# A hybrid decoder layer on one core: the list scheduler's machine model is exchanged

## The chip, the core and the metric

The kernel runs on one core of a Trainium2 chip. The metric is the device time of one execution, in microseconds (us). Of the kernel before there are three runs, with a median of 2636.88 us (2635.72 to 2638.27), and one profiled execution. A core has TensorE (PE, matrix products), VectorE (DVE), ScalarE (ACT) and GpSimd (POOL); SyncE (SP) issues all DMAs of this kernel. Each engine works through its own list of instructions in order; what one engine needs of another it waits for on semaphores.

## The reference

One layer of a decoder, in fp32, for 2048 prompt tokens and 8 x 8 sample tokens that share all weights (model width 1024). Cut to what matters:

```python
q, k, v, u = split(rmsnorm(x, g_mix) @ w_in)        # 1024 -> 1280
attn_o = window_attention(q, k, v, sinks)            # 8 heads x 64, 2 kv heads, window 128, ALiBi
pool_o = pool_mix(u, w_pool) * pool_scale            # causal means over 2, 4, 8, 16 tokens
x = x + concat(attn_o, pool_o) @ w_out
h = rmsnorm(x, g_cross)
p = softmax((h @ w_cq) @ mem_k.T / 16)               # 4 heads x 256, 256 memory tokens
x = x + (p @ mem_v) @ w_co
h = rmsnorm(x, g_ffn)
x = x + square(relu(h @ w_up)) @ w_down              # hidden width 4096
y = rmsnorm(x, g_final)
```

The sample tokens have their own window cache, pooling state and memory cache. For the prompt, mem_k and mem_v are computed from mem_prompt. Keys, values and pooling states are returned too.

## The kernel before

**Precision.** Each fp32 operand of a large product is split into a rounded part "hi" and a remainder "lo", and the product is three passes: hi x hi, hi x lo, lo x hi (L111 to L113 in `mm3`, L280 to L282 in `dense`). The split of a weight tile is made on the core: a DMA brings 512 KB into a staging tile (L131), ScalarE rounds it (L132), VectorE subtracts (L133). That is done 330 times.

**Weights.** The class `Stream` holds a list of all weight tiles in the order of use. `pump` emits the loads and splits ahead of their use, up to five tiles, as far as staging tiles (six) and weight tiles (twelve) are free.

**Activations** lie transposed: features in the partitions, tokens in the columns. The tokens are worked through in three superblocks of two blocks each, of 384 columns (320 or 256 in the last). All tiles are allocated once and handed out by small free lists while the program is traced, so who reuses which buffer after whom is fixed by the traced program.

**Stages.** The prologue warms TensorE up (14 small matmuls of an identity with a tile of ones, L367), splits the memory tokens, computes mem_k and mem_v, and folds w_cq into mem_k and w_co into mem_v, writing the folded matrices to DRAM. Then for each superblock: the input projection interleaved with the window attention, w_out, cross attention with the folded matrices, the MLP in eight groups of 512 hidden channels. In the last superblock the sample tokens have an attention (`attn_sample`) and a cross attention (`sample_cross`) of their own, which reads the sample caches by 512 KB transfers.

**The dense loop.** `dense` goes over output chunks of 128 channels and the two blocks. A chunk for one block is 24 passes into one of four PSUM banks (`MM`). `order` says which chunk of which block comes when: the first `head` chunks run for block 0 and then for block 1, likewise the last `tail`.

**Norms.** For each finished chunk of a residual, VectorE adds (L892, L1093 or L1164), ScalarE squares (L205) and GpSimd adds the square to an accumulator (L206). `Norm.fin` then sums the accumulator over the partitions with a matmul of ones (L214), takes Ln and Exp (L217, L218), three operations on VectorE (L219 to L221), and `Norm.apply` makes the normalised hi and lo parts in eight pieces (L232, L233, L235; the last on VectorE and GpSimd by turns). `fin` is put in a list `later` and traced one chunk after the block's last chunk. Its matmul is the only instruction of the kernel with `keep_in_program_order`, which puts it behind the TensorE instruction that was traced just before it; what is traced after it may still be put ahead of it.

**Attention.** For each tile of 128 queries and each kv head: scores (L676), mask and maximum (L677), Exp, division, transposes by TensorE (L707), probabilities times values (L724, L725). These steps are written as stages with lags, and the generators `attn` and `ug` (the input projection) are traced in turns by `mix`.

**What sets the order.** The traced program is a first order. When the `TileContext` closes, the framework's scheduler makes each engine's list: it is a list scheduler that plays the program on a model of the machine, and takes, for an engine that is free, the earliest traced instruction whose inputs and buffers are ready in that model. So an instruction that waits in the model is passed by others that are traced behind it. How far the lists differ from the traced order depends on what the model takes for the length of each instruction and transfer. The context is opened in `kernel` at L1317.

## Time and profile before

| | |
|---|---|
| median of three runs | 2636.88 us |
| profiled execution, span from first to last instruction | 2632.9 us |
| busy: TensorE, VectorE, ScalarE, GpSimd | 2565.7, 1304.3, 982.1, 665.8 us |
| mean granted TensorE clock | 0.992 of full speed |
| moved by DMA | 244.76 MB, 93 GB/s over the span |

The profile gives no time of its own for the profiled execution outside its span; the span is 4.0 us under the median of the runs. In a row of the timeline stand the start, the length, the engine, the line of the kernel, the operation, the tile it writes and the tiles it reads, how many instructions are merged in the row, and in brackets the idle time before it with what ended it. Matmuls overlap, so a matmul's length in a row is not the distance to the next one; that distance is read from the starts. A row of stretches gives each engine's busy time between two points of the span. "Granted clock" is the share of TensorE's full clock in a stretch.

### The profile page before, as it was taken

To read this page: it belongs to the slowest core of one execution; us is meant where nothing else is said; L and a number is where in the kernel's file an instruction comes from. 1 tells how busy PE (TensorE), PEld (TensorE's weight loads), DVE (VectorE), ACT (ScalarE), POOL (GpSimd) and SP (SyncE) were. 2 spreads that over 40 slices of the span, in tenths; PEclk is the share of its full clock that TensorE was granted. 3 is DMA by queue.
4 is the path that set the end of the run, shared out by engine and by line. 5 is a ranking of instruction groups with operands and counts; after the bars stand their busy time and mean duration, and the time that the engine had idled before them with its cause. 6 is when DMAs were issued, how large, how long until landed. Compare 5 with 4: busy or idle time off the path is not lost. (4 is left out here: it accounts for less than half of the span.)

```text
span 2632.9 us, 39258 instructions
## 1 busy us (share of the span) xinstructions
PE 2565.7 (97%) x15753; PEld 2461.6 (93%) x15753; DVE 1304.3 (50%) x2283; ACT 982.1 (37%) x1923; POOL 665.8 (25%) x723
## 2 busy tenths in 40 slices
PE   8899999999999999999999999999999999999998
PEld 8799989999999999997999999999999669999998
DVE  7567453533333367936363333334766646344334
ACT  6666342422222244824342222223354434322231
POOL 2215322311111153433241111113324214111111
PEclk9999999999999999999999999999999999999999
DMA  7843211211111123131111111112414473222210
GB/s 276 257 130 104 71 47 64 73 65 64 65 65 64 56 70 108 55 123 57 65 63 60 63 64 64 65 57 70 141 60 146 178 269 117 81 81 83 87 57 37
DMA packets 92539, 244.76 MB, mean 93 GB/s; under 512 B 16772, under 2 KB 31556, under 8 KB 91204
## 3 DMA queue, kind: packets, MB, share of 16 engines
q1 hardware_dynamic: 92356, 242.25, 27.0%
q8 instruction: 123, 2.02, 0.3%
q14 instruction: 60, 0.49, 0.1%
HBM read 219.53 MB, written 22.69 MB: 92 GB/s over the span
## 5 line engine op out<-in xcount | busy, mean ns | idle before, releaser
L280 PE MATMUL mm<-act,w 128*128 128x384 f32 (+2 forms) x2784 | 903.0, 324 | 2.6 <-ACT act L631 1.6
L281 PE MATMUL mm<-act,w 128*128 128x384 f32 (+2 forms) x2784 | 897.7, 322 | 0.7 <-DVE act L632 0.5
L282 PE MATMUL mm<-act,w 128*128 128x384 f32 (+2 forms) x2784 | 897.1, 322 | 1.2 <-DVE w L133 1.2
L132 ACT CAST w<-f 128x1024 fp32r<-128x1024 f32 x330 | 346.0, 1050 | 734.7 <-PE mm L112 459.7
L133 DVE TENSOR_TENSOR w<-f,w 128x1024 fp32r<-128x1024 f32 x330 | 425.3, 1294 | 304.7 <-ACT w L132 304.5
L111 PE MATMUL mm<-act,w 128*128 128x384 f32 (+2 forms) x1728 | 552.4, 320 | 9.3 <-ACT w L132 7.6
L113 PE MATMUL mm<-act,w 128*128 128x384 f32 (+2 forms) x1728 | 549.2, 318 | 0.5 <-DVE w L133 0.5
L112 PE MATMUL mm<-act,w 128*128 128x384 f32 (+2 forms) x1728 | 548.9, 318 | 0.0
L280 PEld LDWEIGHTS mm<-act,w 128*128 128x128 f32 x2784 | 527.6, 189 | 7.4 <-issue 2.6
L281 PEld LDWEIGHTS mm<-act,w 128*128 128x128 f32 x2784 | 527.3, 189 | 7.3 <-issue 2.6
L282 PEld LDWEIGHTS mm<-act,w 128*128 128x128 f32 x2784 | 527.2, 189 | 2.0 <-DVE w L133 1.7
L1131 POOL TENSOR_TENSOR t<-t 128x384 f32<-128x384 f32 (+2 forms) x192 | 216.2, 1126 | 1039.5 <-ACT t L1130 1039.5
L1164 DVE TENSOR_TENSOR x<-mm,x 128x384 f32<-128x384 f32 (+2 forms) x384 | 199.8, 523 | 327.9 <-PE mm L113 327.9
L111 PEld LDWEIGHTS mm<-act,w 128*128 128x128 f32 x1728 | 327.2, 189 | 11.3 <-ACT w L132 7.6
L112 PEld LDWEIGHTS mm<-act,w 128*128 128x128 f32 x1728 | 327.1, 189 | 1.0
L113 PEld LDWEIGHTS mm<-act,w 128*128 128x128 f32 x1728 | 327.0, 189 | 0.8 <-DVE w L133 0.8
L206 POOL TENSOR_TENSOR t<-t,t 128x384 f32<-128x384 f32 (+2 forms) x161 | 191.4, 1190 | 344.7 <-ACT t L205 311.7
L1134 DVE TENSOR_TENSOR act<-t,act 128x384 fp32r<-128x384 f32 (+2 forms) x192 | 102.9, 536 | 305.4 <-ACT act L1133 305.4
L1133 ACT CAST act<-t 128x384 fp32r<-128x384 f32 (+2 forms) x192 | 93.4, 487 | 235.3 <-POOL t L1131 235.3
L205 ACT ACTIVATE t<-x 128x384 f32<-128x384 f32 (+2 forms) x140 | 68.3, 498 | 153.1 <-DVE x L1093 75.6
L1130 ACT ACTIVATE t<-mm 128x384 f32<-128x384 f32 (+2 forms) x192 | 88.3, 460 | 93.2 <-PE mm L282 91.9
L111 PE MATMUL mm<-w,act 128*128 128x512 f32 x288 | 117.1, 409 | 3.0 <-ACT w L132 2.7
(187 smaller groups left out, 2211.8 us busy)
## 6 DMA issues: line engine op xcount, KB each, us to landing
f<-in_wup SPq DMA_DIRECT2D x96, 512.0 KB, 3.5
f<-in_wdn SPq DMA_DIRECT2D x96, 512.0 KB, 3.5
f<-in_win SPq DMA_DIRECT2D x30, 512.0 KB, 3.7
f<-a_s SPq DMA_DIRECT2D x24, 512.0 KB, 3.3
f<-b_s SPq DMA_DIRECT2D x24, 512.0 KB, 4.2
x<-in_x SPq DMA_DIRECT2D x6, 1536.0 KB, 7.0
f<-in_wco SPq DMA_DIRECT2D x16, 512.0 KB, 5.5
f<-in_cmk SPq DMA_DIRECT2D x16, 512.0 KB, 4.5
```

The costliest lines, as they stand in the source:

```text
L111: nc.tensor.matmul(ps, Wh(k), Hh(k), start=first and i == 0, stop=False)
L112: nc.tensor.matmul(ps, Wh(k), Hl(k), start=False, stop=False)
L113: nc.tensor.matmul(ps, Wl(k), Hh(k), start=False, stop=final and i == last)
L132: nc.scalar.copy(th[:], r[:, 0:1024])
L133: eng.tensor_tensor(tl[:], r[:, 0:1024], f32(th[:]), ALU.subtract)
L206: self.add.tensor_tensor(self.acc[:, 0:n], self.acc[:, 0:n], t[:, 0:n], ALU.add)
L280: nc.tensor.matmul(ps[:, 0:n], w8(th)[:, k, :], hi(b, k), start=k == 0, stop=False)
L281: nc.tensor.matmul(ps[:, 0:n], w8(th)[:, k, :], lo(b, k), start=False, stop=False)
L282: nc.tensor.matmul(ps[:, 0:n], w8(tl)[:, k, :], hi(b, k), start=False, stop=k == 7)
L1131: nc.gpsimd.tensor_tensor(q[:, 0:n], r[:, 0:n], r[:, 0:n], ALU.mult)
L1134: nc.vector.tensor_tensor(lo, q[:, 0:n], f32(hi), ALU.subtract)
L1164: nc.vector.tensor_tensor(bl.x(m), ps[:, 0:n], bl.x(m), ALU.add)
```

## The change

The `TileContext` is opened with `schedule_with_timeline_sim=True`. The list scheduler then plays the traced program on the framework's timeline model of the machine instead of its default model. Instructions, tiles, buffers, engines and the dependences between instructions stay as they are. The lists of all five engines, the order in which SP issues its DMAs, and the places of the waits can differ.

```diff
-    with tile.TileContext(nc) as tc:
+    with tile.TileContext(nc, schedule_with_timeline_sim=True) as tc:
         tile_hybrid_step_kernel(tc, io)
```

## The prediction

> **What bounds the kernel now.** I read the page first (who is busy), then the busy time by stage (where TensorE is not), then the list of TensorE's waits (what holds it up), then the timeline at the longest wait and at the start.
>
> ```profile
> span 2632.9 us, 39258 instructions
> PE 2565.7 (97%) x15753; PEld 2461.6 (93%) x15753; DVE 1304.3 (50%) x2283; ACT 982.1 (37%) x1923; POOL 665.8 (25%) x723
> 0.00:230.00 230.00, 211.53 (x1341) 196.90 (x1342) 167.10 (x354) 154.99 (x331) 58.39 (x82) 0.99 0.58 193
> 470.00:930.00 460.00, 459.64 (x2650) 459.38 (x2651) 165.51 (x228) 122.99 (x193) 79.47 (x70) 1.00 0.19 64
> 1350.00:1830.00 480.00, 480.00 (x2771) 479.95 (x2770) 178.74 (x254) 131.70 (x212) 86.79 (x78) 1.00 0.19 63
> 1920.00:2010.00 90.00, 84.01 (x579) 78.36 (x579) 67.04 (x193) 58.17 (x165) 37.67 (x64) 0.94 0.29 100
> 2010.00:2210.00 200.00, 189.41 (x1301) 151.69 (x1300) 106.06 (x183) 81.59 (x152) 56.11 (x61) 0.99 0.53 188
> 2210.00:2600.00 390.00, 389.96 (x2907) 389.69 (x2906) 159.60 (x253) 113.45 (x197) 71.06 (x70) 1.00 0.21 73
> 2600.00:2633.00 33.00, 22.43 (x152) 20.46 (x151) 14.79 (x34) 6.92 (x16) 4.16 (x5) 0.89 0.19 73
> ```
>
> After the bounds and the length of a stretch stand the busy times of PE, PEld, DVE, ACT and POOL, then granted clock, DMA share, GB/s. TensorE is idle for 2632.9 - 2565.7 = 67.2 us in all. The three long dense stretches, 460 + 480 + 390 = 1330 us, hold 0.4 us of it: half of the kernel has nothing that an order can fill. At the end, 10.6 us of 33 are the drain behind the last matmuls. What an order can touch is in the other stages: prologue, attention, the stage boundaries, the sample group's cross attention. There TensorE waits for this:
>
> ```profile
> PE aux L214 <- POOL t L206: 20.7, 9, 3.7
> PE mm L111 <- ACT w L132: 10.3, 3, 7.6
> PE aux L676 <- DVE st L677: 2.8, 6, 0.9
> ```
>
> The three numbers are the total in us, the times, and the longest. Of the second row 7.6 us are the wait for the first data. The first row is the largest: the matmul that sums a norm's squares over the partitions, held up nine times, by up to 3.7 us, by GpSimd's last addition.
>
> **The part that decides: order.** The diff changes no instruction, only the model of the machine on which the scheduler finds out what is ready when. So I look for places where the present order shows that its model was wrong about this chip. A list scheduler that knew of a wait would have put ready work into it. At the longest wait it did not:
>
> ```profile
> 466.16 0.33 PE L281 MATMUL mm<-act,w 128*128 128x384 f32 x1
> 466.34 0.34 PE L282 MATMUL mm<-act,w 128*128 128x384 f32 x1
> 470.36 0.91 PE L214 MATMUL aux<-t,ones 128*128 128x384 f32 x2 [3.69 <-POOL t L206]
> 470.82 0.63 PE L280 MATMUL mm<-act,w 128*128 128x384 f32 x1
> 463.86 4.00 DVE L133 TENSOR_TENSOR w<-f,w 128x1024 fp32r<-128x1024 f32 x2
> 467.78 0.55 DVE L1093 TENSOR_TENSOR x<-mm,x 128x384 f32<-128x384 f32 x1
> 468.25 1.21 DVE L133 TENSOR_TENSOR w<-f,w 128x1024 fp32r<-128x1024 f32 x1
> 468.42 0.52 ACT L205 ACTIVATE t<-x 128x384 f32<-128x384 f32 x1 [3.39 <-DVE x L1093]
> 464.78 2.00 POOL L206 TENSOR_TENSOR t<-t,t 128x384 f32<-128x384 f32 x1
> 469.09 1.22 POOL L206 TENSOR_TENSOR t<-t,t 128x384 f32<-128x384 f32 x1 [2.31 <-ACT t L205]
> ```
>
> The 24 passes of the first w_up chunk end at 466.34, L214 follows in its traced place at 470.36, and the next chunk starts right behind it: block 0's activations had been in use for 24 passes, so it was ready. The chain that L214 waits for is DVE's residual add (467.78, itself behind two weight subtractions), ACT's square, POOL's addition. The model of before must have had that chain done earlier, or TensorE later. The start shows the same from the other side:
>
> ```profile
> 1.01 0.29 POOL masks.py:199 TENSOR_SCALAR_AFFINE_SELECT ident<-ident 128x128 f32<-128x128 f32 x1
> 7.57 0.58 PE L111 MATMUL mm<-act,w 128*128 128x256 f32 x1 [7.57 <-ACT w L132]
> ...
> 9.43 0.41 PE L112 MATMUL mm<-act,w 128*128 128x256 f32 x1
> 9.64 5.62 PE L367 MATMUL aux<-ident,ones 128*128 128x128 f32 x28
> 15.02 0.36 PE L113 MATMUL mm<-act,w 128*128 128x256 f32 x1
> 15.22 0.28 PE L111 MATMUL mm<-act,w 128*128 128x256 f32 x1
> 15.34 0.29 PE L112 MATMUL mm<-act,w 128*128 128x256 f32 x1
> 8.69 2.46 DVE L380 SCALAR_TENSOR_TENSOR act<-x,vec,act 128x256 fp32r<-128x256 f32 x6
> 11.93 1.22 DVE L133 TENSOR_TENSOR w<-f,w 128x1024 fp32r<-128x1024 f32 x1
> ```
>
> The warm-up passes (L367) are traced ahead of every weight matmul and need only the identity, which is complete at 1.01 + 0.29 = 1.30 us. Five L111/L112/L113 matmuls (first and last shown) were put ahead of them, so they run from 9.64 to 15.0, in front of real work, where from 1.3 to 7.57 they would be free.
>
> **Term 1, warm-up.** If it goes first, L113 need not wait till 15.02. It is then paced by DVE: the last input piece is there at 8.69 + 2.46 = 11.15 and the second chunk's subtraction ends at 11.93 + 1.22 = 13.15. The first chunk's 19 remaining passes (0.12 us each, 15.22 to 15.34) would be over by about 11.5, the second is bound by 13.15; now the first ends at 15.02 + 19 x 0.12 = 17.3. Gain 17.3 - 13.15 = 4.2 us; the bounds are 0 (the model again takes the identity for late) and the whole 5.4 us from 9.64 to 15.02.
>
> **Term 2, the norm sums.** Upper bound 20.7 us. Lower bound 0.4 us per wait, by what is late next: a gap filled at L214 brings TensorE sooner to the block whose norm was being summed. After 470.82 come three chunks of block 0, 72 passes x 0.173 us (466.16 to 466.34) = 12.5 us, and 21 more until the last piece of the other block is used, at 486.9 us. That piece is ready at
>
> ```profile
> 485.48 1.02 POOL L235 TENSOR_TENSOR act<-t,act 128x384 fp32r<-128x384 f32 x1 [1.04 <-ACT act L233]
> ```
>
> that is 486.5: slack 0.4 us. TensorE 3.7 us early would wait 3.3 us there, unless the 24 passes of the following group's first chunk (4.2 us) move ahead too; their weights are prefetched and four matmul banks exist. I take 60% of 20.7 = 12.4 us, nearer to the upper end because the same rule that fills the first gap fills the second.
>
> **Term 3, the clock.** Six times the granted clock falls just after such waits; first and last of the six stretches:
>
> ```profile
> 75.00:100.00 25.00, 22.08 (x137) 19.95 (x137) 19.52 (x23) 17.82 (x32) 10.71 (x7) 0.93 0.80 263
> 2200.00:2225.00 25.00, 21.86 (x152) 20.89 (x151) 20.70 (x32) 12.80 (x29) 14.29 (x14) 0.93 0.20 64
> ```
>
> Each costs 25 x 0.07 = 1.75 us; with half of them gone, 3 x 1.75 = 5.2 us; bounds 0 and 10.5. [...]
>
> **Term 4, the rest.** The idle time left is 67.2 - 7.6 (start) - 10.6 (end) - 20.7 = 28.3 us, in pieces of a few tenths in attention, mostly behind DVE, and in the sample group's cross attention, behind transfers. I bound it by half of it gained (14 us) and by the loss of the DVE rival below, and take nothing. The moved DMA issues on SP's queue I cost at nothing in the dense stages: DMA engines are 0.19 busy there, and no row of the waits above names a transfer. Without that cover a late 512 KB weight tile costs up to what the sample stage idles, 10.6 us in 200.
>
> **Sum.** 4.2 + 12.4 + 5.2 = 21.8 us. 2632.9 - 21.8 = 2611.1 us of span. The profiled span stands 4.0 us under the median of the runs, 2636.9, and the same distance above the new span gives 2615.
>
> **Rivals.** *Nothing moves that counts.* TensorE's order is already right in the 1330 us of dense work, and if the new model too has the norm chain done in time, the waits stay: 2637. For it: the wait arises partly from two subtractions that took 4.00 us where one alone takes 1.21, and a model need not know of that. Against it: the misplaced warm-up shows that the models have something to differ in.
>
> *Slower: DVE becomes the bound in attention.* Place: the three attention stretches, of which the second shows
>
> ```profile
> 1075.00:1100.00 25.00, 24.02 (x153) 22.14 (x152) 22.96 (x73) 20.20 (x60) 12.64 (x19) 1.00 0.04 12
> 1100.00:1125.00 25.00, 24.53 (x144) 23.04 (x143) 24.38 (x50) 20.59 (x44) 17.14 (x19) 1.00 0.46 165
> 1075.00:1100.00 25.00, 1.04 (x1) 1.00 0.04 12
> 1100.00:1125.00 25.00, 7.33 (x7) 1.00 0.46 165
> L133 DVE TENSOR_TENSOR w<-f,w 128x1024 fp32r<-128x1024 f32 x330 | 425.3, 1294 | 304.7 <-ACT w L132 304.5
> ```
>
> (the last two stretch rows are L133 alone). DVE is busy 22.96 and 24.38 of 25 us, third number. Now one weight subtraction lies in the first of these and seven in the next, at the stretch's end. A scheduler that sees a weight tile ready earlier puts its subtraction into any small gap of DVE, ahead of the softmax reductions that TensorE's next transposes wait for. Six moved in at 1.294 us are 7.8 us per stretch, 23 us for three: 2660 with nothing gained, 2638 beside the forecast's gain. It decides from the point where DVE's free time is used up, 25 - 22.96 = 2.0 us in the first row, that is from the second moved subtraction on. [...]
>
> *Slower by broken accumulation.* If the new model shows a gap between the passes of one chunk, the scheduler weaves several chunks together; four banks then fill at the same moment and TensorE waits for an evacuation, some 1 us per four chunks of 4.2 us, 6% of 1330 us: 2715. Nothing in the trace speaks for it.
>
> **How the numbers follow.** A measurement of this kernel can tell about 0.2%, 5.3 us, from no change. Chances: forecast 0.55, nothing 0.15, DVE 0.22, broken accumulation 0.08. The forecast's own range is 2588 (5.4 + 20.7 + 10.5 + 14 = 50.6 us gained) to 2631. The range over the cases goes up to 2658, about the DVE rival without gain, and leaves out the fourth case and the edges. Faster 0.55, within 0.2% 0.15, slower 0.30.
>
> **What would show it.** Right: L367 ahead of the first L111, complete before 8 us; the L214 row of TensorE's waits under 9 us; more stretches at clock 1.00; dense stretches as full as before. Term 2 is wrong if L280 or L111 <- POOL/DVE L235 appears with what L214 lost. The DVE rival is right if L676 and L707 waits grow in attention with more L133 there. The forecast is wrong as a whole if TensorE's idle time does not fall below 55 us.

## The result and the profile after

The changed kernel takes 2671.2 us (median of 4 runs, 2670.9 to 2672.2), the kernel before 2636.3 us beside it: a ratio of 1.0139 with a 95% interval of 1.0126 to 1.0151. It is 35 us slower by the medians, 37 by the ratio. The forecast was 2615 us, faster.

The page of the changed kernel, its first lines:

```profile
span 2669.8 us, 39258 instructions
PE 2582.8 (97%) x15753; PEld 2471.2 (93%) x15753; DVE 1300.7 (49%) x2283; ACT 984.6 (37%) x1923; POOL 662.0 (25%) x723
```

The instructions are the same in number. TensorE is idle for 2669.8 - 2582.8 = 87.0 us instead of 67.2, which is 19.8 us of the 36.9 us of span. The other 17.1 us are "busy" time: the same 15753 matmuls took 2582.8 us instead of 2565.7. The mean granted clock fell from 0.992 to 0.984; 0.016 of 2669.8 us are 43 us missing, 0.008 of 2632.9 us were 21. So in this execution the added idle time counts nearly twice: once by itself and once as a lower clock behind it. That is no fixed factor. In the last kernel of the experiments idle time falls by 10.0 us and busy time by 0.1.

What TensorE waits for in the changed kernel (total, times, longest):

```profile
PE mm L113 <- DVE act L235: 14.2, 5, 4.5
PE mm L281 <- DVE act L235: 5.4, 4, 2.8
PE mm L111 <- ACT w L343: 5.2, 1, 5.2
PE aux L111 <- ACT act L96: 5.0, 1, 5.0
PE mm L282 <- DVE w L133: 4.0, 5, 2.1
PE aux L676 <- DVE st L677: 3.8, 11, 0.8
PE mm L111 <- ACT w L132: 3.8, 3, 2.5
PE aux L214 <- POOL t L206: 0.2, 1, 0.2
```

The L214 row, 20.7 us before, is down to 0.2; in its place stand two rows of L235, the last step of the same norm, with 14.2 + 5.4 = 19.6 us. Beside these are two new single waits of 5 us, in the prologue's last fold (L343) and in the sample group's cross attention (L96).

The dense stretches in the changed kernel (bounds, length, busy PE, PEld, DVE, ACT, POOL, clock, DMA share, GB/s) are as full as they were; the first two hold 0.7 us of idle time, and the third is busy for all of the 380 us from 2260 on, so nothing was lost there:

```profile
480.00:940.00 460.00, 459.34 (x2650) 459.02 (x2650) 169.68 (x231) 124.93 (x196) 83.81 (x72) 1.00 0.20 62
1380.00:1840.00 460.00, 460.00 (x2655) 459.95 (x2654) 167.60 (x237) 124.76 (x199) 78.38 (x70) 1.00 0.20 66
```

The start, and the norm of the second block behind the first output projection, in the changed kernel's timeline:

```profile
1.36 5.40 PE L367 MATMUL aux<-ident,ones 128*128 128x128 f32 x28 [1.36 <-POOL ident masks.py:199]
9.03 0.58 PE L113 MATMUL mm<-act,w 128*128 128x256 f32 x1 [0.76 <-DVE w L133]
...
324.67 1.33 POOL L206 TENSOR_TENSOR t<-t,t 128x384 f32<-128x384 f32 x1 [0.64 <-ACT t L205]
333.79 0.39 PE L113 MATMUL mm<-w,act 128*128 128x512 f32 x1
334.01 0.81 PE L214 MATMUL aux<-t,ones 128*128 128x384 f32 x2
347.36 0.79 PE L113 MATMUL mm<-w,act 128*128 128x512 f32 x1 [4.52 <-DVE act L235]
```

The warm-up now lies in the wait for the first data, and L113 comes at 9.03 us instead of 15.02. At the norm, GpSimd's last addition is over at 326.0, but L214 comes at 334.0, 8 us late: behind cross-attention matmuls, 29 of them traced after it. Those 29 belong to two later chunks, whose passes the new list weaves into those of the chunk before the sum. Before, TensorE waited 1.4 us there and the sum went at once. Now there is no wait at L214, but the norm's pieces come late and the next matmuls that need them wait 4.5 us, at 347.

### The profile page after: what moved, and what is told of

It reads as the page before. It is cut to its first block, busy times and chain, and to the rows that moved or that the text cites. A ratio compares the mean times of both kernels' runs of the same rounds, so it can differ in the third digit from the quotient of the medians.

```text
span 2669.8 us, 39258 instructions
## 1 busy us (share of the span) xinstructions
PE 2582.8 (97%) x15753; PEld 2471.2 (93%) x15753; DVE 1300.7 (49%) x2283; ACT 984.6 (37%) x1923; POOL 662.0 (25%) x723
## 4 chain that ended last, share of the span: by engine, by line
PE 85%; DVE 8%; DMA 3%; ACT 2%; issue 1%; POOL 1%; SPq 0%; DVEq 0%; ACTq 0%; POOLq 0%
PE mm L281 15%; PE mm L282 15%; PE mm L280 15%; PE mm L113 12%; PE mm L111 12%; PE mm L112 11%; DVE t L232 2%; DVE w L133 1%; DVE x L677 1%; PE aux L676 1%; ACT w L132 1%; DMA f<-in_cmv 1%; DMA f<-in_wco 1%; PE aux L707 1%; PE aux L214 0%
## 5 line engine op out<-in xcount | busy, mean ns | idle before, releaser
L281 PE MATMUL mm<-act,w 128*128 128x384 f32 (+2 forms) x2784 | 899.2, 323 | 7.1 <-DVE act L235 5.4
L133 DVE TENSOR_TENSOR w<-f,w 128x1024 fp32r<-128x1024 f32 x330 | 415.3, 1262 | 326.8 <-ACT w L132 321.4
L113 PE MATMUL mm<-act,w 128*128 128x384 f32 (+2 forms) x1728 | 549.9, 318 | 0.8 <-DVE w L133 0.8
L281 PEld LDWEIGHTS mm<-act,w 128*128 128x128 f32 x2784 | 527.9, 190 | 11.8 <-DVE act L235 6.5
L1164 DVE TENSOR_TENSOR x<-mm,x 128x384 f32<-128x384 f32 (+2 forms) x384 | 200.3, 523 | 333.7 <-PE mm L113 333.6
L113 PEld LDWEIGHTS mm<-act,w 128*128 128x128 f32 x1728 | 326.9, 189 | 1.5 <-DVE w L133 1.2
L113 PE MATMUL mm<-w,act 128*128 128x512 f32 x288 | 116.1, 407 | 14.2 <-DVE act L235 14.2
```

Of the source, the lines that this page charges most:

```text
L113: nc.tensor.matmul(ps, Wl(k), Hh(k), start=False, stop=final and i == last)
L133: eng.tensor_tensor(tl[:], r[:, 0:1024], f32(th[:]), ALU.subtract)
L281: nc.tensor.matmul(ps[:, 0:n], w8(th)[:, k, :], lo(b, k), start=False, stop=False)
L1164: nc.vector.tensor_tensor(bl.x(m), ps[:, 0:n], bl.x(m), ALU.add)
```

## The experiments

For most kernels a helper was added that runs once the program is traced and ties neighbours of a given list together by order-only edges, so that an engine must take its instructions in that list. The traced program, the tiles and the computation stay the same. "A" is the list of an engine in the changed kernel, "B" in the kernel before.

```diff
     with tile.TileContext(nc) as tc:
         tile_hybrid_step_kernel(tc, io)
+        _pin(tc, nc, LISTS)
```

Gains and losses in us below are the ratio to the kernel before on the same chip, less 1, times 2635. "Cover" is independent work that is ready and that an engine can do while something else is waited for.

**One engine's list or the others'.**

```diff
+LISTS = {"PE": A["PE"]}
```

> TensorE executes exactly the changed kernel's list; the other four engines are ordered by the default model around it. Theory A (the loss lies in TensorE's own list: instructions that are not ready are passed by some 23 to 63 matmuls, so that their followers come late, and independent matmuls that should cover the waits of attention and of the sample group are spent early): 2665 to 2675 us, ratio 1.011 to 1.014, with the L235 waits of TensorE at about 20 us and half-clock time near 85 us. Rival B (the loss lies in the order of weight splits and norm steps on VectorE, ScalarE and GpSimd, or in SyncE's order of loads): 2636 to 2645 us, since those lists then come from the default model again. Both in part: in between, and the split is read from it.

Measured: 2696.8 us, ratio 1.0234 (1.0218 to 1.0250), +62 us.

```diff
-    with tile.TileContext(nc) as tc:
+    with tile.TileContext(nc, schedule_with_timeline_sim=True) as tc:
...
+LISTS = {"PE": B["PE"]}
```

> The mirror image: TensorE executes exactly the list of the kernel before, the other four engines are ordered by the timeline model around it. Theory A: 2630 to 2642 us, ratio 0.998 to 1.002, the L214 waits back at about 20 us. Rival B: 2660 to 2671 us.

Measured: 2675.6 us, ratio 1.0155 (1.0139 to 1.0171), +41 us. Both theories fall. The first mixture is slower than both kernels, and the second is no faster than the changed one: TensorE's list and those of the other engines are made for each other, and the loss can't be put on one engine. From here on whole stretches were exchanged, all five lists at once.

**Stretch by stretch.**

```diff
+LISTS = B, with the 14 L367 of PE ahead of the first L111
```

> All five lists as in the kernel before, only the 14 warm-up passes (L367) put ahead of the first weight matmul on TensorE. The prediction's first term: 4.2 us less, 2632 us, ratio 0.998 to 0.999, and the first L113 at about 10 to 11 us instead of 15.02. Rival (the time is paced by the input weights from memory and by the splits on VectorE behind them, so an earlier start is handed to the next wait): within 1 us of before, with a longer wait at L111 or L113 between 10 and 70 us.

Measured: ratio 0.9996 (0.9987 to 1.0004), -1 us (-3.4 to +1.1).

```diff
+LISTS = B up to the second group's MLP, A from there
```

> All five lists of the kernel before up to the middle of the second token group's MLP, where both kernels agree, and the changed kernel's lists from there to the end (third group's attention, output projection, cross attention and MLP). If losses are local to their stage (theory A), the landmarks of the changed kernel give 36.8 - 10.1 = 26.7 us here: 2660 to 2664 us, ratio 1.009 to 1.011, of which about 15 us between the last step of the third group's cross projection and the end of its cross attention. Rival (the third group's loss comes from loads or matmul banks displaced in earlier groups): under 10 us here.

Measured: 2659.6 us, ratio 1.0094 (1.0078 to 1.0111), +25 us, as the first reading had it.

```diff
+LISTS = A up to the first fold, B from there
```

> All five lists of the changed kernel up to the first fold of the prologue (the product of the cross query weight), those of the kernel before from there on. In the changed kernel TensorE's 750th matmul started 11.9 us earlier than before, its 825th only 2.3. Theory (the fold of the output weight is paced by its loads, and the dense work that could have covered them was done early): 0 to 4 us less than before, 2630 to 2634 us, with a wait at the fold's tiles of 5 us or more about 120 us. Rival (the loss at 121 us comes from the changed order in the fold and the attention behind it, which this kernel does not have): 9 to 12 us less, 2623 to 2626 us.

Measured: 2628.2 us, ratio 0.998 (0.997 to 0.999), -5 us: between the two. The order of the prologue is a gain. The loss at 121 us belongs to the new order from the first fold on, which this kernel doesn't have: its 750th matmul is 8.0 us ahead of the kernel before and its 800th 7.9, but in the changed kernel these are 11.8 and 2.2. There the fold of the pooling weight into the output weight waits for its scaled weight (L343), and the clock falls. The wait, then the stretch around it in the kernel before and in the changed kernel:

```profile
122.70 0.80 PE L111 MATMUL mm<-w,w 128*128 128x512 f32 x1 [5.25 <-ACT w L343]
120.00:140.00 20.00, 18.86 (x101) 17.36 (x100) 11.06 (x18) 13.53 (x25) 1.18 (x4) 1.00 0.78 244
120.00:140.00 20.00, 16.37 (x65) 14.43 (x66) 9.94 (x15) 12.05 (x21) 2.21 (x4) 0.74 0.57 175
```

No run put the order of this fold alone into the kernel before.

```diff
+LISTS = A in the three stretches from input projection to attention, B elsewhere
```

> All five lists of the kernel before, but in the three stretches from the input projections to the end of attention the changed kernel's. The landmarks of the changed kernel lose some 5 us there in the first group, 4 in the second and none in the third. If these losses belong to the order in the stretch itself: 7 to 11 us more than before, 2641 to 2646 us, with more TensorE wait at L676 and L707. Rival (they were brought in by loads and banks from the stretch before): within 2 us of before.

Measured: 2655.2 us, ratio 1.0071 (1.0056 to 1.0086), +19 us (15 to 23), more than either reading. In its execution, 21.0 us behind at the end of the MLP, 9.1 us arise in the second stretch (from 5.3 to 14.4 in the table below) and 5.7 in the first (2.8 ahead at the 800th matmul, 2.9 behind at the 1500th). The third adds about 2, and what is left arises where its lists are those of the kernel before, 2.6 of it as one drop of the clock.

```diff
+LISTS = A from output projection to MLP in groups one and two, B elsewhere
```

> All five lists of the kernel before, but the changed kernel's in the first and the second group from the output projection through the cross attention to the MLP's first half. If the losses belong to their stretches: 8 to 14 us more than before (the landmarks of the changed kernel lose some 2 to 5 us per group between the output projection's first step and the MLP, once the attention's loss is taken off), 2641 to 2648 us. With prologue (-5), attention (+21) and third group (+25) the four parts would then exceed the whole (+37), so parts would not add. Rival (additive): the rest, 37 + 5 - 21 - 25 = -4, within 5 us of before.

Measured: ratio 1.0004 (0.9995 to 1.0013), +1 us, as the additive rival had it. The sum of the parts is near the whole: -5 + 19 + 1 + 25 = 40 us, against 37 (33 to 40). That the parts add is not shown by it: the four kernels have the third group's attention twice and the prologue's last fold, where the changed kernel loses 9.6 us in one execution, in none, and each part is known to 2 to 4 us.

Where the differences arise within one execution of each, in us against the kernel before. The rows are the start of the first or the end of the last instruction of a line: L387 in the prologue, L892 behind the output projection, L1093 behind the cross projection, L1164 behind the MLP. Executions of the same lists differ too: up to group 2's MLP the last column has the lists of the kernel before, and yet runs from -3.2 to +2.0.

| point | before at | changed | prologue | attention | cross | third group |
|---|---|---|---|---|---|---|
| last L387 | 67.2 | -6.7 | -7.1 | -0.3 | -0.4 | -1.2 |
| group 1, first L892 | 266.5 | +2.1 | -8.3 | +0.7 | -1.7 | -3.2 |
| group 1, first L1093 | 399.5 | +5.6 | -6.5 | +2.7 | +3.1 | -1.5 |
| group 1, last L1164 | 1007.0 | +4.5 | -4.1 | +5.3 | +1.4 | +0.8 |
| group 2, first L892 | 1141.8 | +8.6 | -3.6 | +14.4 | +2.0 | +1.5 |
| group 2, first L1093 | 1275.3 | +13.6 | -3.8 | +14.2 | +4.9 | +1.1 |
| group 2, last L1164 | 1882.6 | +10.5 | -3.7 | +15.8 | +1.6 | +2.0 |
| group 3, first L892 | 2004.5 | +10.3 | -6.7 | +15.8 | -1.0 | +4.4 |
| group 3, last L892 | 2051.0 | +13.0 | -6.9 | +17.6 | -1.0 | +7.1 |
| group 3, last L1093 | 2205.6 | +33.0 | -5.3 | +20.2 | +5.5 | +24.3 |
| group 3, last L1164 | 2622.9 | +36.8 | -5.3 | +21.0 | +6.6 | +27.7 |

The 2 to 3 us between group 1's rows of L1093 and L1164 (prologue, attention, third group) are one drop of the clock, which the last section shows for the third.

**The norm sums.** First the changed kernel with eight L214 put back. What was traced before a sum runs ahead of it again, so for most of them matmuls that were woven with later ones move too:

```diff
-LISTS["PE"] = A["PE"]
+LISTS["PE"] = A["PE"] with the 63, 29, 25, 29, 25, 20, 23, 43 matmuls traced after eight L214, and run ahead of them, put behind them
```

> All five lists of the changed kernel, except that eight of its norm sums (L214: the first group's first norm, the norms of the second token block behind the output projection and behind the cross projection of all groups, and one behind the second MLP) are put back to their traced place among the matmuls around them: 20 to 63 matmuls that were traced later and went ahead now come behind. Theory A1 (each norm sum that was ready after 2 to 4 us came 2 to 8 us late, and the block's later steps with it): the changed kernel loses 5 us between the output projection and the next one in each of the first two groups and some 15 in the third; 18 to 25 of the 36 us come back, 2646 to 2653 us, L235 waits of TensorE from 20 us to under 5, L214 waits from 0.2 to 10 or more. Rival A2 (the cover is what is short: what is gained for the norm is lost again as a wait at L214, or the waits sit elsewhere): under 6 us back, 2665 to 2672 us.

Measured: 2704.9 us, ratio 1.0264 (1.0251 to 1.0277), +70 us; 34 us slower than the changed kernel, where 18 to 25 less were expected. The L113 row of L235 rose to 18.9 us. The four other lists had been made for late sums; that this is why it lost, as with the exchanged engine lists, was not tried by itself. Either way this run does not price a late sum. The next two change the sums in lists that fit otherwise. The number of matmuls that pass a sum is called its dose, and it fits when they just fill the wait:

```diff
+LISTS["PE"] = B["PE"] with nine L214 put 11, 6, 20, 6, 6, 20, 11, 3, 17 places behind
```

> All five lists of the kernel before, except that the nine norm sums (L214) at which TensorE waits 1.4 to 4 us are each passed by just as many matmuls as fit into that wait: 11, 6, 20, 6, 6, 20, 11, 3 and 17. This is the prediction's second term by itself. As predicted: 12 us less (9 to 20), 2614 to 2625 us, ratio 0.992 to 0.997. Its lower bound (what was filled is handed to the next step of the same chain, the last piece of the normalised block at L235): 1 to 4 us less, 2630 to 2634 us, with as much wait at L235 as the L214 row lost.

```diff
+LISTS["PE"] = B["PE"] with nine L214 put 22, 18, 40, 20, 18, 40, 22, 9, 43 places behind
```

> The same edit as in the kernel with the waiting norm sums filled, with all five lists of the kernel before, but each of the nine is passed by about twice as many matmuls or more: 22, 18, 40, 20, 18, 40, 22, 9 and 43 instead of 11, 6, 20, 6, 6, 20, 11, 3 and 17. The 132 matmuls too many at 0.173 us are 22.8 us by which the norms come late. Theory A1, in a form in which no other list is changed (a norm that comes late is handed on to the steps behind it): 8 to 17 us more than with filled waits, 2636 to 2645 us, with waits at L235. Rival A2 (there is cover enough behind the norms, only the right dose gains and a double dose neither gains nor loses): 2626 to 2633 us.

Measured: 2627.9 us, ratio 0.998 (0.9969 to 0.9992), -5 us (-8 to -2) with the fitting dose; 2641.4 us, ratio 1.0024 (1.0013 to 1.0035), +6 us with the double one. TensorE's waits with the fitting dose, then with the double one:

```profile
PE aux L919 <- POOL cp L943: 5.9, 4, 2.6
PE aux L214 <- POOL t L206: 4.0, 7, 1.2
PE mm L281 <- DVE act L235: 2.6, 4, 0.8
PE mm L281 <- POOL act L235: 1.8, 3, 0.6
PE mm L113 <- DVE act L235: 1.1, 4, 0.4
```

```profile
PE aux L919 <- POOL cp L943: 9.6, 8, 3.1
PE mm L281 <- POOL act L235: 3.6, 5, 1.2
PE mm L281 <- DVE act L235: 3.2, 6, 0.8
```

Filling the waits takes 16.7 us off the L214 row, but 4.4 us of new waits stand at L281 (2.6 + 1.8), and those for cross attention's copies (L943) rise from 2.0 to 5.9. Idle time falls by 3.5 us only, from 67.2 to 63.7; busy time falls by another 3.4, from 2565.7 to 2562.3, with the clock at 0.995 instead of 0.992. With 132 matmuls too many, 22.8 us of lateness, the waits move on to the next steps, and 12 us are lost against the fitting dose. Idle time is then 66.8 us, only 3.1 more; most of the loss is busy time, 2572.0 us, at a clock of 0.992. So a late sum is handed on, and the dose decides the sign. In the changed kernel's list six of the nine sums are passed by 63, 29, 29, 20, 23 and 43 matmuls, where 11, 6, 6, 11, 3 and 17 fit.

**Attention.** Matmuls of the projections (tile mm) in the second attention stretch, kernel before, then the kernel with only the attention's order changed, at bounds 5 us later since it is there that much behind. The count in the first brackets, TensorE's matmuls, is what matters:

```profile
1040.00:1060.00 20.00, 15.17 (x75) 12.30 (x73) 4.06 (x7) 3.46 (x6) 1.00 0.08 27
1060.00:1080.00 20.00, 15.42 (x70) 11.93 (x70) 4.23 (x7) 3.95 (x7) 1.00 0.13 41
1080.00:1100.00 20.00, 14.44 (x70) 11.70 (x69) 2.05 (x3) 2.70 (x5) 1.00 0.05 14
1100.00:1120.00 20.00, 16.73 (x85) 14.61 (x84) 2.35 (x4) 3.77 (x7) 1.00 0.35 120
```

```profile
1045.00:1065.00 20.00, 17.35 (x87) 14.36 (x86) 4.32 (x7) 3.79 (x7) 1.00 0.15 49
1065.00:1085.00 20.00, 18.07 (x86) 14.28 (x85) 3.29 (x6) 3.87 (x7) 1.00 0.02 6
1085.00:1105.00 20.00, 9.12 (x36) 6.50 (x36) 2.04 (x3) 2.22 (x4) 0.91 0.06 14
1105.00:1125.00 20.00, 15.13 (x66) 11.21 (x66) 2.04 (x3) 3.19 (x6) 1.00 0.14 40
```

Before, the projections are spread evenly beside the softmax, 70 to 85 in each 20 us. In the new order 173 instead of 145 come in the first 40 us, and 36 instead of 70 in the next 20; the 9 us are lost from there on. The order spent the cover first. VectorE has no more splits there than before: 4 L133 in these 80 us against 6. Whether VectorE, busy for 37.2 of the last 40 us, is then the bound was tried with a cheaper L133, which leaves out the low part of the weights, in the lists of the kernel before and in those with the attention's order changed:

```diff
-            eng.tensor_tensor(tl[:], r[:, 0:1024], f32(th[:]), ALU.subtract)
+            eng.tensor_copy(tl[:], r[:, 0:1024])
```

> The reference for the next kernel: the kernel before with its five lists, but each weight's low part (L133, VectorE, 330 times, 1.29 us) is a plain copy of the unsplit weight, one input instead of two, so the low part of the weights is left out. The duration of a copy is to be read from this run. Both theories: 0 to 10 us less than before, since VectorE is off the path in the dense stretches.

> The lists of the kernel with the changed kernel's order in the three attention stretches, with the same plain copy in place of L133 (the low part of the weights is left out). In the second attention stretch that order loses 9 us against before; VectorE is 6.4 us less busy there between 1040 and 1080 us, and full from 1090 on. Theory V (TensorE ran its projections, which need little of VectorE, first, and VectorE's work was left for a time in which it is the bound): with VectorE's work lightened by some 0.5 us or more per weight, the second stretch loses 4 us or less against light_before. Rival L (TensorE waits for the latency of the chain of softmax, which no lighter weight split shortens, since the projections that should cover it are gone): still 7 to 10 us.

Measured: 2607.1 us, ratio 0.9904 (0.9889 to 0.9919), and 2623.2 us, 0.9961 (0.9947 to 0.9975). The copy's row in the first, against 425.3 us and 1294 ns for the subtraction:

```profile
L133 DVE CAST w<-f 128x1024 fp32r<-128x1024 f32 x330 | 247.2, 752 | 174.6 <-PE mm L282 135.0 <-DMA f<-in_wco 14.9 <-DMA f<-in_win 5.9
```

Against each other they are still 15 us apart (19 with the subtraction), and in the second stretch 8.8 us (9.1 before): light_before gains 4.1 us on the kernel before there, light_attention loses 4.7. Theory V falls for this stretch, and L stands: the loss stays however light the splits are. That it is cover that is missing rests on the counts and on the fall of V; no run moved the projections alone. The copy also doesn't wait for ScalarE's high part, so its gain holds both costs of the split. Its own result was outside what was expected: with the copy the kernel before is 25 us faster, most of it in prologue and attention.

**The third group.** The sample tokens' chain, in the kernel before and then in the one with the third group's order changed: the last addition of the output projection, the norm sum, the query's transposes, the first matmuls with sample keys.

```profile
2050.56 0.48 DVE L892 TENSOR_TENSOR x<-mm,x 128x320 f32<-128x320 f32 x1
2053.82 0.81 PE L214 MATMUL aux<-t,ones 128*128 128x320 f32 x2 [0.97 <-POOL t L206]
2075.94 0.46 PE L983 MATMUL aux<-ident,f 64*128 64x64 f32 x4
2078.02 1.94 PE L1002 MATMUL aux<-f,f 128*32 128x256 f32 x24
```

```profile
2057.66 0.48 DVE L892 TENSOR_TENSOR x<-mm,x 128x320 f32<-128x320 f32 x1
2068.95 0.70 PE L214 MATMUL aux<-t,ones 128*128 128x320 f32 x2
2101.78 0.71 PE L983 MATMUL aux<-ident,f 64*128 64x64 f32 x8
2103.93 1.94 PE L1002 MATMUL aux<-f,f 128*32 128x256 f32 x24
```

The chain is 7.1 us late at its first row, 15.1 at the second (GpSimd's sum was ready 8.6 us before), 25.8 and 25.9 at the last two: at each step matmuls of the other block went ahead. The end of the cross projection is 24.3 us late. Transfers were the rival cause, as the DMA share is 0.88 to 0.93 from 2150 to 2180 us in the second of these kernels:

```diff
-                        nc.sync.dma_start(kk[:, 0:1024], io["cmk"][4 * bg + b, hh])
+                        nc.sync.dma_start(kk[:, 0:512], io["cmk"][4 * bg + b, hh][:, 0:512])
...
-                                             kk[:, 256 * (i % 4):256 * (i % 4) + 256], start=b == 0 and db == 0, stop=b == 3 and db == 1,
+                                             kk[:, 256 * (i % 2):256 * (i % 2) + 256], start=b == 0 and db == 0, stop=b == 3 and db == 1,
```

and the same for `cmv`, in the lists of the kernel before and in those with the third group's order changed.

> The reference for the next kernel: the lists of the kernel before, but the sample group's keys and values (in_cmk, in_cmv) are loaded and used in half of their columns only, 256 KB instead of 512 KB for each of the 32 tiles, so the other half is left out of the computation. Both theories: 0 to 12 us less than before, all of it between the last step of the third group's output projection and its MLP; SyncE's loads were up to 0.95 of the transfer capacity there.

> The lists with the changed kernel's order in the third group, with the same halved loads. At full loads that order starts the first key load at 2085 us instead of 2071, has TensorE use up the other block's matmuls meanwhile, and loses 25 us. Theory D (from 2110 us on the transfers are the bound, and TensorE waits for them without cover): with half the bytes, 8.4 MB less or some 26 us at the 320 GB/s of that stretch, the loss against half_loads_before falls to 12 us or less. Rival N (the late norm sum and the query projection behind it cost their 14 us by themselves, whatever the loads take): the loss stays at 18 to 27 us.

Measured: ratio 0.9992 (0.9983 to 1.0001), -2 us, and 1.0087 (1.0073 to 1.0101), +23 us; 25 us apart, as with full loads. D falls. In the second of them TensorE is idle or at low clock while the DMA share is 0.77 and 0.70 (next to last number; 0.93 and 0.91 in these 20 us with full loads):

```profile
2160.00:2170.00 10.00, 5.17 (x52) 1.62 (x44) 1.23 (x1) 2.49 (x3) 0.00 (x0) 0.71 0.77 244
2170.00:2180.00 10.00, 6.09 (x19) 3.41 (x20) 5.66 (x6) 4.89 (x7) 0.00 (x0) 0.61 0.70 248
```

The longest wait of TensorE from 2100 to 2200 us, with full loads and then with half, is one for a step of the sample tokens' own chain and no transfer:

```profile
PE aux L111 <- ACT act L96: 4.9, 1, 4.9
PE aux L111 <- ACT act L96: 6.3, 1, 6.3
```

What stands is N, the late chain, with its cover used up by 2160 us. The steps are read from the trace; no run made the chain late by itself.

**A version that is faster than both.**

```diff
+LISTS = A up to the first fold, B from there, with eight L214 put 6, 20, 6, 6, 20, 11, 3, 17 places behind
```

> The two changes that gained by themselves, together: the changed kernel's five lists up to the first fold of the prologue (5.3 us less), and from there those of the kernel before with eight waiting norm sums (L214) passed by as many matmuls as fit into their waits (5.3 us less with nine). If they add up: 2621 to 2625 us, ratio 0.995 to 0.997. Rival (both gains end in the same later wait, the sample group's loads, where the warm-up's 3.8 us also went): 2627 to 2630 us.

Measured: 2623.4 us, ratio 0.996 (0.9947 to 0.9972), 11 us less than before (7 to 14) and 48 less than the changed kernel. The two gains add up. Its page's first lines:

```profile
span 2622.8 us, 39258 instructions
PE 2565.6 (98%) x15753; PEld 2457.0 (94%) x15753; DVE 1303.6 (50%) x2283; ACT 980.5 (37%) x1923; POOL 665.8 (25%) x723
```

Idle time is 57.2 us instead of 67.2.

## Why the prediction was wrong

**Term 1, the warm-up first, 4.2 us.** Right at its place: L367 runs from 1.36 to 6.76 us, as forecast before 8, and alone it brings 3.8 us as far as the first group's first L892. At the end 1 us (-3.4 to +1.1) is left; in its trace the 4 us were still there at the third group's last L892 and gone at its first L1093. The sum had not allowed for a later stage that takes a gain back.

**Term 2, the norm sums, 12.4 us.** This step failed. The row fell as far as it could, 20.7 to 0.2 us, and the falsifier came true with it: L235 rows of 19.6 us. Two assumptions were wrong. By itself the right dose is worth 5 us, clock included, near the lower end (0.4 us at nine waits, 3.6), because what is filled is handed to the next steps. And "the same rule that fills the first gap fills the second" took it that the scheduler would stop at the gap's size. It passed six of nine sums by 20 to 63 matmuls where 3 to 17 fit, and a double dose is a loss of 6 us.

**Term 3, the clock, 5.2 us.** Wrong in sign: the mean clock fell to 0.984, as waits of up to 5.2 us arose elsewhere. That half of the six drops would go was an estimate, which no run shows. The sign it counted on is seen where the waits were filled with the fitting dose: L214's longest wait fell from 3.7 to 1.2 us, the clock rose from 0.992 to 0.995 and busy time fell by 3.4 us.

**Term 4, the rest, taken as nothing.** The main error. The new orders of attention (+19) and of the third group (+25) each cost that much when put into the kernel before, together more than the whole loss, and both were listed as stages that an order can touch. The sum counted only the gains of a better place for late instructions and gave no price to the cover that is moved to that place. In the changed kernel's own execution the prologue's last fold also takes back 9.6 of the 11.8 us gained ahead of it. That moved cover is what the stages lose by is read from traces; no run shows it alone.

**Rivals.** "Nothing moves" and "broken accumulation" are out: the dense stretches are full, and where passes of several chunks are woven, around the norm sums, the longest waits are for L235 and not for an evacuated bank; the 1 us per four chunks of that rival was an estimate, which no run shows. The slower rival, VectorE as the bound in attention, had the sign, and the place of about half of the loss. Its own mechanism, more splits moved in, is not what costs: the second stretch has no more of them than before, and with splits at 752 ns instead of 1294 its loss stays at 8.8 us. The sentence "wrong as a whole if TensorE's idle time does not fall below 55 us" decides: it is 87.0. One sum of the prediction is off by itself: 50.6 us less than 2636.9 are 2586.3, not the 2588 at which its range begins.

## What to carry to other kernels

A scheduler's new model is not a set of local repairs: where it fills a wait, count the work that it takes for it, ask where that work had been needed, and price the stretch it is taken from. Where independent work is scarce, here in attention and beside the sample chain, the order that spread it evenly beat the one that started it early. The lists of several engines are one schedule; exchange whole stretches of all engines between two kernels, not one engine's list, to find the parts that gain and keep only those.

## What was not expected of the hardware

**One wait, two clocks.** The kernel before and the one with only the third group's order changed have the same lists around 470 us, and the same wait. L214 and the stretch around it, kernel before, then the other:

```profile
470.36 0.91 PE L214 MATMUL aux<-t,ones 128*128 128x384 f32 x2 [3.69 <-POOL t L206]
455.00:490.00 35.00, 31.31 (x179) 30.73 (x178) 29.12 (x37) 16.79 (x34) 19.31 (x16) 1.00 0.14 45
```

```profile
468.81 1.65 PE L214 MATMUL aux<-t,ones 128*128 128x384 f32 x2 [3.69 <-POOL t L206]
455.00:490.00 35.00, 31.31 (x165) 30.39 (x164) 26.10 (x34) 15.30 (x30) 17.79 (x15) 0.90 0.14 45
```

The clock stays at 1.00 in the first and is 0.90 over 35 us in the second, 14 matmuls fewer. That is the shift of 2 to 3 us in the table's row behind group 1's MLP. Of five kernels with this wait in this place, TensorE busy for 31.31 of the 35 us in each, three show 0.90 (those with the prologue's, the attention's or the third group's order changed) and two 1.00 (the kernel before and the one with the warm-up first). In the changed kernel a shorter wait, with another of 0.9 us some 3 us ahead of it, was enough (the wait, and the clock around its end):

```profile
2252.70 0.64 PE L281 MATMUL mm<-act,w 128*128 128x320 f32 x1 [2.81 <-DVE act L235]
2250.00:2255.00 5.00, 2.30 (x9) 2.31 (x10) 5.00 (x9) 2.81 (x8) 3.46 (x4) 0.66 0.00 0
```

So the length of a wait alone doesn't decide: 3.69 us kept the clock at 1.00 in the kernel before, and 2.81 us did not in the changed one. What decides was not shown by any run.

Leaving out 8.4 of the 16.8 MB of keys and values that the sample cross attention loads changed the time by 2 us (-4 to 0).
